# A two-layer diffusion step on one core: gate and up products of three feed-forward stages as seven block products in place of eight

## The chip, the cores and the metric

One Trainium2 chip, one of its cores. The metric is the device time of one launch in microseconds (us); the times shown are medians of runs, and lower is better. TensorE is called PE, VectorE DVE, ScalarE ACT, GpSimd POOL, and SyncE, which issues most transfers, SP. PEld stands for PE's loads of the stationary operand.

## What is computed

A backbone of two layers works on 640 tokens (128 context tokens, 512 latent ones) of 1024 features, all in float32. Each layer is a feed-forward stage, a mixer, and a second feed-forward stage:

```
x <- LN(alpha*x + 0.5*g1*SwiGLU_1(x*(1+s1)+b1))
x <- LN(alpha*x + g2*W_out[RG-LRU | GQA | MLA](x*(1+s2)+b2))
x <- LN(alpha*x + 0.5*g3*SwiGLU_2(x*(1+s3)+b3))

SwiGLU(u) = (silu(u @ w_gate) * (u @ w_up)) @ w_down      w_gate, w_up: 1024 x 2816, w_down: 2816 x 1024
mod = silu(cond) @ w_mod + b_mod                          nine sections of 1024 columns in each layer
```

The gates g, scales s and shifts b are sections of `mod`. There are four feed-forward stages, called f00, f01, f10 and f11 here (layer, then first or second), and two mixers, m0 and m1. The order of the program is f00, m0, f01, f10, m1, f11.

## The kernel before

**Products.** Every float32 operand of a large product is kept as two parts, hi (rounded to the PE's float32r format) and lo (the rest), and a product is three matmuls: hi by hi, hi by lo, lo by hi (`mm3`, lines 516 to 518). An **m-tile** is 128 of the 2816 hidden features, so a stage has 22. For one m-tile the gate product runs over 8 blocks of K and two halves of 320 tokens, three matmuls each, and so does the up product: 2 x 8 x 2 x 3 = 96 matmuls of 128x320. They accumulate in PSUM tiles of two banks (`p2`, three of them). The gate goes through silu on ACT (line 593), is multiplied by the up product on DVE (598) and is split into hi and lo (600, 601).

**Down products.** After every chunk of three or four m-tiles (`CHUNKS`) the function `down` runs ten groups (5 token tiles x 2 halves of the 1024 columns) of three matmuls of 128x512 for each m-tile (lines 809 to 811), in two one-bank PSUM tiles (`p1`). Each group is multiplied by the stage's gate on DVE (815) and added to the residual `x` on POOL (817), in the last chunk on DVE, with the statistics of the layer norm behind it (457).

**Weights.** A weight block of 512 KB is loaded by SP into a ring of `NR` = 4 raw tiles (`raw`), and split: a cast on ACT gives hi (175), a subtraction on DVE gives lo (180). The ring's slot is free after the split. Loads are taken in the order of the steps (`feed`).

**Modulation.** Sections of later stages are computed while a feed-forward stage runs: for each of 8 row blocks of w_mod, four DVE operations of 128x512 (lines 318 and 320). `PLAN` says which stage computes which sections: f00 five, f01 four, f10 four, f11 none; one section each falls into m0 and m1, on PE there.

**Order.** The program is a list of `Step`s. `run` emits the body of a step, and at each of its yields also one of the waiting splits of the next step that has some, so that weights are ready a little ahead; each engine then keeps an order that the framework's scheduler fixes when the kernel is built. At the start of a stage the residual is rescaled on DVE (lines 1916 and 1917), and stored to DRAM only ahead of a mixer (`spill`). At the program's start, 16 small transfers of per-layer vectors (`vrows`, lines 264 to 271) go out on POOL's own queue, while SP issues the loads of x, of the condition vectors (`crow`) and of the first weights.

## Time and profile before

| | |
|---|---|
| time of three runs | 2614.26, 2616.35, 2619.17 us (median 2616.35) |
| profiled execution | span 2615.8 us from first to last instruction; its own time is not listed apart, and its span lies 0.55 us below the median of the runs |
| busy: PE, DVE, ACT, POOL | 97%, 58%, 33%, 25% of the span |
| granted PE clock | full speed (tenths: 9 in each slice) |
| traffic | 272.80 MB, mean 104 GB/s |
| instructions | 39802, of them 16392 matmul records |

How to read it: a matmul's record is longer than the time after which the next one starts, because matmuls are pipelined, so what one costs is the distance between two starts. DVE's records overlap a little in the same way. The table of stretches gives the busy time of each engine by stage.

### The profile page before, as it was taken

The numbers are of one execution on the slowest core, as the hardware profiler recorded it, in microseconds if no ns is written. First come the engines' busy times: TensorE is split into PE (matmuls) and PEld (weight loads), VectorE is DVE, ScalarE is ACT, GpSimd is POOL, SyncE is SP. The second block draws the span as 40 slices with busy tenths as digits, with TensorE's granted clock in tenths as the row PEclk, the third lists the DMA queues.
The fourth block names the chain that finished last, engine by engine and source line by source line (L and its number), as shares of the span: only waits on it lengthen the run. The fifth ranks groups of instructions, "written<-read, shape, count | busy, mean of one in ns | idle before, by whom it ended". The sixth has DMA issues, their size and how long they took to land.

```text
span 2615.8 us, 39802 instructions
## 1 busy us (share of the span) xinstructions
PE 2532.2 (97%) x16392; PEld 2309.0 (88%) x16392; DVE 1519.1 (58%) x2332; ACT 860.3 (33%) x1315; POOL 643.7 (25%) x581
## 2 busy tenths in 40 slices
PE   8899999988999999999999999999999999999997
PEld 7799999888679889999988999998986899999996
DVE  5855765668656755545576636545786565323335
ACT  3312221356772322111242212214657542212211
POOL 4311022126433121121022211022363232210112
PEclk9999999999999999999999999999999999999999
DMA  7634543331221543333324424331330323223211
GB/s 273 187 96 141 160 130 106 92 98 54 88 77 59 173 121 105 100 111 113 114 64 154 126 77 145 114 113 46 99 106 26 114 87 97 73 65 97 73 57 41
DMA packets 266149, 272.80 MB, mean 104 GB/s; under 512 B 13236, under 2 KB 223728, under 8 KB 265968
## 3 DMA queue, kind: packets, MB, share of 16 engines
q1 hardware_dynamic: 265456, 270.18, 33.6%
q8 instruction: 129, 2.11, 0.3%
q14 instruction: 52, 0.43, 0.0%
q0 software_dynamic: 512, 0.08, 0.0%
HBM read 260.30 MB, written 8.34 MB: 103 GB/s over the span
## 4 chain that ended last, share of the span: by engine, by line
PE 57%; DVE 8%; issue 4%; ACT 2%; DMA 2%; POOL 1%; DVEq 0%; POOLq 0%; ACTq 0%; SPq 0%
PE p L516 12%; PE p L517 12%; PE p L518 12%; PE p L809 5%; PE p L810 5%; PE p L811 5%; PE p L1424 3%; PE p L1462 3%; PE p L1496 2%; DVE x L320 1%; DVE x L1916 1%; DVE x L1917 1%; DVE t L815 1%; DMA raw<-in_ffn_w_down 1%; DVE w L180 1%
## 5 line engine op out<-in xcount | busy, mean ns | idle before, releaser
L516 PE MATMUL p<-u,w 128*128 128x320 f32 (+2 forms) x2928 | 910.6, 311 | 2.7 <-ACT uf L502 1.5
L517 PE MATMUL p<-u,w 128*128 128x320 f32 (+2 forms) x2928 | 908.6, 310 | 3.0 <-POOL u L508 2.2
L518 PE MATMUL p<-u,w 128*128 128x320 f32 (+2 forms) x2928 | 907.3, 310 | 1.2 <-DVE w L180 1.2
L817 POOL TENSOR_TENSOR x<-x,t 128x512 f32<-128x512 f32 x200 | 273.7, 1371 | 1229.4 <-DVE t L815 1226.2
L516 PEld LDWEIGHTS p<-u,w 128*128 128x128 f32 x2928 | 552.1, 189 | 9.5 <-issue 2.9
L517 PEld LDWEIGHTS p<-u,w 128*128 128x128 f32 x2928 | 552.1, 189 | 6.4 <-POOL u L508 3.9
L518 PEld LDWEIGHTS p<-u,w 128*128 128x128 f32 x2928 | 552.0, 189 | 1.9 <-DVE w L180 1.8
L175 ACT CAST w<-raw 128x1024 fp32r<-128x1024 f32 x211 | 221.9, 1051 | 750.5 <-PE p L517 531.6
L180 DVE TENSOR_TENSOR w<-raw,w 128x1024 fp32r<-128x1024 f32 x211 | 263.0, 1248 | 222.1 <-ACT w L175 218.9
L809 PE MATMUL p<-dw,b 128*128 128x512 f32 x880 | 347.1, 394 | 14.8 <-DVE t L815 14.8
L810 PE MATMUL p<-dw,b 128*128 128x512 f32 x880 | 343.1, 390 | 0.0
L811 PE MATMUL p<-dw,b 128*128 128x512 f32 x880 | 342.7, 390 | 0.0
L320 DVE SCALAR_TENSOR_TENSOR x<-raw,cst,x 128x512 f32<-128x512 f32 x364 | 274.5, 805 | 48.4 <-DMA raw<-in_w_mod 48.0
L815 DVE TENSOR_TENSOR t<-p,g 128x512 f32<-128x512 f32 x240 | 164.6, 686 | 230.8 <-PE p L811 227.6
L175 ACT CAST dw<-raw 128x1024 fp32r<-128x1024 f32 x90 | 92.7, 1051 | 559.8 <-PE p L810 426.0
L809 PEld LDWEIGHTS p<-dw,b 128*128 128x128 f32 x880 | 165.2, 188 | 59.2 <-DVE t L815 24.7
L598 DVE TENSOR_TENSOR b<-b,p 128x640 f32<-128x640 f32 (+2 forms) x89 | 70.9, 796 | 222.4 <-PE p L518 222.2
L811 PEld LDWEIGHTS p<-dw,b 128*128 128x128 f32 x880 | 165.2, 188 | 35.2 <-DVE b L601 0.3
L810 PEld LDWEIGHTS p<-dw,b 128*128 128x128 f32 x880 | 165.3, 188 | 32.1
L180 DVE TENSOR_TENSOR dw<-raw,dw 128x1024 fp32r<-128x1024 f32 x90 | 118.6, 1328 | 112.7 <-ACT dw L175 112.7
L1487 POOL TENSOR_SCALAR b<-b,sm 128x640 f32<-128x640 f32 x96 | 78.3, 817 | 143.2 <-DVE sm L1477 60.6
L1476 DVE TENSOR_REDUCE sm<-p 128x1 f32<-128x640 f32 x96 | 78.9, 821 | 56.3 <-PE p L1462 52.9
(325 smaller groups left out, 3249.0 us busy)
## 6 DMA issues: line engine op xcount, KB each, us to landing
raw<-in_w_mod SPq DMA_DIRECT2D x132, 512.0 KB
raw<-in_ffn_w_gate SPq DMA_DIRECT2D x88, 512.0 KB
raw<-in_ffn_w_up SPq DMA_DIRECT2D x88, 512.0 KB
raw<-in_ffn_w_down SPq DMA_DIRECT2D x88, 512.0 KB
raw<-in_w_in SPq DMA_DIRECT2D x26, 512.0 KB
raw<-in_w_out SPq DMA_DIRECT2D x16, 512.0 KB
wm<-in_w_mod SPq DMA_DIRECT2D x12, 512.0 KB
xd<-x SPq DMA_DIRECT2D x10, 512.0 KB
```

The costliest lines, as they stand in the source:

```text
L175: nc.scalar.copy(h, hold["raw"])
L180: nc.vector.tensor_sub(l, hold["raw"], f(hold["hi"]))
L320: e.scalar_tensor_tensor(acc[:, cs], hold["raw"][:, cs], c, acc[:, cs], op0=ALU.mult, op1=ALU.add)
L516: nc.tensor.matmul(out, lhsT=wh, rhs=xh, start=start, stop=False)
L517: nc.tensor.matmul(out, lhsT=wh, rhs=xl, start=False, stop=False)
L518: nc.tensor.matmul(out, lhsT=wl, rhs=xh, start=False, stop=stop)
L809: nc.tensor.matmul(pt, lhsT=hh[:, ts], rhs=d["hi"][:, hsl], start=(i == 0), stop=False)
L810: nc.tensor.matmul(pt, lhsT=hh[:, ts], rhs=d["lo"][:, hsl], start=False, stop=False)
L811: nc.tensor.matmul(pt, lhsT=hl[:, ts], rhs=d["hi"][:, hsl], start=False, stop=(i == len(ms) - 1))
L815: nc.vector.tensor_mul(tt, pt, gt[h])
L817: e.tensor_add(x[:, hsl], x[:, hsl], tt)
L1476: nc.vector.tensor_reduce(st[:, 0:1], v, axis=AX.XY, op=ALU.max, negate=True)
```

## The change

Three stages (f01, f10, f11) are built by a new function `ffn_fast`; f00 keeps the old one. In `ffn_fast` the first two m-tiles (`CLASSIC` = 2) are computed as before. For the other 20, the 1024 inputs (K) are cut in two halves, the 640 tokens in two halves of 320, and the pair (gate, up) is the third cut, so that an m-tile is a 2 x 2 by 2 x 2 block product, done in **seven** block products of 4 blocks of K x 320 tokens (84 matmuls for 96). It needs sums of blocks of u once a stage (`sums`, `third`), four differences of weight halves for each m-tile, in place in the raw tiles on POOL (`prep`), splits of half the old width, and additions of results in PSUM (`keep_x`, `keep_q`, `fix`, `up1`). Weights are split up to three steps ahead (`LOOK`). Down products always follow three m-tiles (the last four) and are summed in SBUF tiles `acc`; the gate and the residual, which is now stored to DRAM in every stage, come in once, by `blend`, on POOL. Of the sections of modulation f00 now computes seven, f01 and f10 three each, f11 one and m1 none. The ring has five raw tiles, and the 16 transfers of `vrows` move from POOL's queue to ACT's.

```diff
-NR = 4
+NR = 5
 PLAN = {
-    "f00": [[], [], [(0, 3), (0, 4), (0, 5), (0, 6), (0, 7)]],
+    "f00": [[], [], [(0, 3), (0, 4), (0, 5), (0, 6), (0, 7), (1, 0), (1, 1)]],
-    "f01": [[], [], [(1, 0), (1, 1), (1, 2), (1, 3)]],
-    "f10": [[], [], [(1, 4), (1, 5), (1, 6), (1, 7)]],
-    "m1": [[], [(1, 8)]],
-    "f11": [[], [], []],
+    "f01": [[], [], [(1, 2), (1, 3), (1, 4)]],
+    "f10": [[], [], [(1, 5), (1, 6), (1, 7)]],
+    "m1": [[], []],
+    "f11": [[], [], [(1, 8)]],
+NX = 8
+LOOK = 3
+CLASSIC = 2
...
-            nxt = next((todo[k] for k in range(i + 1, len(steps)) if steps[k].splits), deque())
+            near = [todo[k] for k in range(i + 1, min(len(steps), i + 40)) if steps[k].splits][: s.look]
...
-            q = nc.gpsimd
+            q = nc.scalar
...
+    def ffn_fast(self, l, j, mods):
...
+                def whole(h, ts):
+                    t = B().rearrange("p (k n) -> p k n", k=2)
+                    nc.gpsimd.tensor_add(t, f(uh[h][:, ks, ts]), f(ul[h][:, ks, ts]))
+                    return t
...
+        def prep(m, key):
...
+            def op():
+                nc.gpsimd.tensor_sub(at(src), at(sub[0]), at(sub[1]))
+
+            def hi():
+                w = pairs[m, key] = self.W([P, 2, 4, P])
+                nc.scalar.copy(w[:, 0], at(src))
+
+            def lo():
+                w = pairs[m, key]
+                nc.vector.tensor_sub(w[:, 1], at(src), f(w[:, 0]))
+                if key in ("U2", "T4"):
+                    self.raw_out -= 1
...
+        def product(m, key, q, start, after=None, extra=()):
...
+                for k in range(4):
+                    xh, xl = a(k)
+                    out = bank(m, q)
+                    for i, (a1, b1) in enumerate(((w[:, 0, k], xh), (w[:, 0, k], xl), (w[:, 1, k], xh))):
+                        nc.tensor.matmul(
...
+            def keep_x():
+                tmp[m] = B()
+                nc.scalar.copy(tmp[m][:, H0], bank(m, X))
+
+            def keep_q():
+                nc.scalar.copy(tmp[m][:, H1], bank(m, Q))
+
+            def fix():
+                nc.vector.tensor_add(bank(m, Z), bank(m, Z), tmp[m][:, H0])
+                nc.scalar.copy(tmp[m][:, H0], bank(m, Z))
+                nc.vector.tensor_add(bank(m, Q), bank(m, Q), tmp[m][:, H0])
+
+            return [
+                product(m, "G1", X, True, keep_x, extra.get(0, ())),
+                product(m, "T1", Q, True, keep_q, extra.get(1, ())),
+                product(m, "T2", Z, True, fix, extra.get(2, ())),
+            ]
...
+            def up1():
+                nc.vector.tensor_add(tmp[m][:, H1], bank(m, Z), tmp[m][:, H1])
...
+            return [
+                product(m, "G2", X, False, gate0, extra.get(0, ())),
+                product(m, "T3", Z, False, up1, extra.get(1, ())),
+                product(m, "U2", Q, False, h0, extra.get(2, ())),
+                product(m, "T4", Z, False, h1, extra.get(3, ())),
+            ]
...
+        def blend():
...
+                    nc.sync.dma_start(out=xin, in_=env["x_d"][t][:, cs])
+                    yield
+                    nc.gpsimd.tensor_mul(acc[t][:, cs], acc[t][:, cs], g[:, cs])
+                    yield
+                    nc.gpsimd.tensor_add(acc[t][:, cs], acc[t][:, cs], xin)
...
+                        if begin:
+                            nc.scalar.copy(x[:, cs], pt)
+                        elif last:
+                            tt = T()
+                            nc.vector.tensor_mul(tt, pt, env["gate"][1 if t == 0 else 0][:, cs])
+                            nc.vector.tensor_add(x[:, cs], x[:, cs], tt)
+                            self.ln_part(t, h, 2)
+                        else:
+                            nc.vector.tensor_add(x[:, cs], x[:, cs], pt)
...
+        while n + 2 < NM:
+            a, b, c = n, n + 1, n + 2
...
+            S += part_a(a, {2: dw[0:1]} if n > CLASSIC else {})
+            S += part_a(b, {0: dw[1:2], 2: dw[2:3]} if n > CLASSIC else {2: dw})
+            S += mods.get(a, [])
+            S += part_b(a)
+            S += part_a(c)
+            S.append(down([a - 2, a - 1, a], begin=n == CLASSIC))
+            if n + 5 >= NM:
+                S.append(Step([], [], start_blend))
+            S += mods.get(b, [])
+            S += part_b(b) + mods.get(c, []) + part_b(c)
+            n += 3
```

Three places of the order show what moves. The number behind a name is its buffer; [waits ...] names what the instruction waits for, DMAHWn being the n-th of eight marks that transfers of SP and ACT take in turn.

First, SP's queue at the program's start. Before:

```order
L281 DMA x_78<-in_x_sample 128x512
L281 DMA x_79<-in_x_sample 128x512
L231 DMA crow<-in_c 8x128
L232 DMA crow<-in_c_ctx 8x128
L233 DMA crow<-in_b_mod 16x128
L170 DMA raw_150<-in_ffn_w_gate 128x8x128 [waits DMAHW0_49]
L1963 DMA wm_130<-in_w_mod 128x2x512 [waits DMAHW1_49]
L1963 DMA wm_131<-in_w_mod 128x2x512 [waits DMAHW2_49]
L1963 DMA wm_132<-in_w_mod 128x2x512 [waits DMAHW3_49]
L1963 DMA wm_133<-in_w_mod 128x2x512 [waits DMAHW4_49]
```

and now:

```order
L285 DMA x_77<-in_x_sample 128x512
L285 DMA x_78<-in_x_sample 128x512 [waits DMAHW0_49]
L285 DMA x_79<-in_x_sample 128x512 [waits DMAHW3_49]
L235 DMA crow<-in_c 8x128 [waits DMAHW5_49]
L236 DMA crow<-in_c_ctx 8x128 [waits DMAHW7_49]
L237 DMA crow<-in_b_mod 16x128 [waits DMAHW1_49]
L173 DMA raw_150<-in_ffn_w_gate 128x8x128 [waits DMAHW3_49]
L2344 DMA wm_130<-in_w_mod 128x2x512 [waits DMAHW0_49]
L2344 DMA wm_131<-in_w_mod 128x2x512 [waits DMAHW2_49]
L2344 DMA wm_132<-in_w_mod 128x2x512 [waits DMAHW3_49]
```

Before, nine transfers go out with no wait, and the first weight load is the first that waits. Now ACT's 16 transfers take marks from the same eight, and SP waits from its fourth transfer on, `crow` and the weights behind it.

Second, DVE between two down chunks. Before, in f01 (180 lo of a weight block, 598 and 601 the hidden features, 374 the end of a modulation section):

```order
L598 TENSOR_TENSOR b_8848<-b_8848,p_1274_9046 128x640
L180 TENSOR_TENSOR w_9204<-raw_9148,w_9188 128x1024
L601 TENSOR_TENSOR b_9109<-b_8848,b_9108 128x640
L180 TENSOR_TENSOR w_9293<-raw_9206,w_9279 128x1024
L180 TENSOR_TENSOR dw_9622<-raw_9357,dw_9604 128x1024
L598 TENSOR_TENSOR b_9119<-b_9119,p_1289_9175 128x640
L374 TENSOR_TENSOR modsb_9260<-p_1299_9251,bm_97 128x256
```

and now, in f11 (1048 lo of a half block, 1101 and 1103 `fix`, 1117 `up1`, 1120 and 1125 the hidden features, 324 modulation):

```order
L1048 TENSOR_TENSOR w_22191<-raw_21943,w_22191 128x512
L1101 TENSOR_TENSOR p_2926_21036<-p_2926_21036,b_22117 128x320
L1048 TENSOR_TENSOR w_22204<-raw_21943,w_22204 128x512
L1103 TENSOR_TENSOR p_2925_21035<-p_2925_21035,b_22117 128x320
L324 SCALAR_TENSOR_TENSOR x_21164<-raw_22168,cst,x_21164 128x512 x2
L324 SCALAR_TENSOR_TENSOR x_21165<-raw_22168,cst,x_21165 128x512 x2
L1048 TENSOR_TENSOR w_22234<-raw_21818,w_22234 128x512
L1101 TENSOR_TENSOR p_2926_21036<-p_2926_21036,b_22182 128x320
L1048 TENSOR_TENSOR w_22250<-raw_22210,w_22250 128x512
L1103 TENSOR_TENSOR p_2925_21035<-p_2925_21035,b_22182 128x320
L1117 TENSOR_TENSOR b_22117<-p_2926_21036,b_22117 128x320
L1048 TENSOR_TENSOR w_22270<-raw_22210,w_22270 128x512
```

The half blocks' splits now stand between the additions in PSUM, and PE's T4 waits for 1117, PE's next products for 1101 and 1103.

Third, POOL ahead of the last down chunk of f01. Before it only added the chunk to x:

```order
L817 TENSOR_TENSOR x_7626<-x_7626,t_9030 128x512
L817 TENSOR_TENSOR x_7626<-x_7626,t_9043 128x512
L817 TENSOR_TENSOR x_7618<-x_7618,t_9469 128x512
L817 TENSOR_TENSOR x_7618<-x_7618,t_9482 128x512
L817 TENSOR_TENSOR x_7620<-x_7620,t_9495 128x512
```

and now (1040 differences of weight halves, 1145 the gate's factor 0.5, 1155 and 1157 `blend`):

```order
L1040 TENSOR_TENSOR raw_11754<-raw_11781,raw_11754 128x512
L1145 TENSOR_SCALAR x_12029<-x_12029 128x1024
L1040 TENSOR_TENSOR raw_11754<-raw_11754 128x512
L1155 TENSOR_TENSOR x_9150<-x_9150,x_12029 128x512
L1157 TENSOR_TENSOR x_9150<-x_9150,t_12036 128x512
L1155 TENSOR_TENSOR x_9150<-x_9150,x_12029 128x512
...
L1155 TENSOR_TENSOR x_9154<-x_9154,x_12026 128x512
L1157 TENSOR_TENSOR x_9154<-x_9154,t_12199 128x512
L1040 TENSOR_TENSOR raw_11796<-raw_11905,raw_11796 128x512
L1040 TENSOR_TENSOR raw_11905<-raw_11905 128x512
```

The twenty operations of `blend` stand as one block, with the differences of m-tile 20 (the last two rows) behind them.

## Rows read from the trace of the kernel before

**Rows 1.** The page's busy line: engine, busy us, share, instructions.
```profile
PE 2532.2 (97%) x16392; PEld 2309.0 (88%) x16392; DVE 1519.1 (58%) x2332; ACT 860.3 (33%) x1315; POOL 643.7 (25%) x581
```
**Rows 2.** Stretches f00, f01, f10, f11: length; busy PE, PEld, DVE, ACT, POOL; PEclk, DMA.
```profile
0.00:530.00 530.00, 507.46 (x3351) 462.90 (x3351) 339.01 (x518) 139.46 (x189) 118.83 (x114) 1.00 0.47 146
...
855.00:1340.00 485.00, 475.79 (x2886) 442.03 (x2885) 281.27 (x384) 121.62 (x159) 88.94 (x71) 0.99 0.37 113
1340.00:1821.00 481.00, 474.21 (x2885) 441.27 (x2884) 277.19 (x381) 117.92 (x156) 88.10 (x72) 1.00 0.37 110
...
2142.00:2602.00 460.00, 458.85 (x2753) 430.82 (x2751) 183.07 (x222) 101.27 (x118) 81.79 (x66) 1.00 0.24 74
```
**Rows 3.** Timeline of PE, gate products in f00: start, length, instruction.
```profile
299.74 0.31 PE L516 MATMUL p<-u,w 128*128 128x320 f32 x1
...
305.90 0.31 PE L516 MATMUL p<-u,w 128*128 128x320 f32 x1
```
**Rows 4.** Timeline of PE, down products in f01.
```profile
980.28 0.39 PE L809 MATMUL p<-dw,b 128*128 128x512 f32 x1
...
984.36 0.39 PE L809 MATMUL p<-dw,b 128*128 128x512 f32 x1
```
**Rows 5.** Groups of DVE: operation, shapes, count | busy us, mean ns | idle before.
```profile
L180 DVE TENSOR_TENSOR w<-raw,w 128x1024 fp32r<-128x1024 f32 x211 | 263.0, 1248 | 222.1 <-ACT w L175 218.9
L815 DVE TENSOR_TENSOR t<-p,g 128x512 f32<-128x512 f32 x240 | 164.6, 686 | 230.8 <-PE p L811 227.6 <-POOL x L817 3.1
...
L601 DVE TENSOR_TENSOR b<-b,b 128x640 fp32r<-128x640 f32 x86 | 70.8, 824 | 1.6 <-ACT b L600 1.6
...
L1849 DVE TENSOR_TENSOR b<-p,b 128x256 f32<-128x256 f32 x40 | 16.8, 419 | 13.2 <-PE p L518 9.8 <-issue 3.1
```
**Rows 6.** Groups of ACT.
```profile
L506 ACT CAST u<-uf 128x512 fp32r<-128x512 f32 x50 | 30.9, 618 | 1.3
...
L1525 ACT CAST b<-p 128x256 fp32r<-128x256 f32 x24 | 9.1, 378 | 5.1 <-PE p L1424 5.1
```
**Rows 7.** Groups of POOL.
```profile
L817 POOL TENSOR_TENSOR x<-x,t 128x512 f32<-128x512 f32 x200 | 273.7, 1371 | 1229.4 <-DVE t L815 1226.2 <-DVE spt L1056 1.9 <-DVE spt L1053 1.2
...
L2016 POOL TENSOR_TENSOR u<-b,u 128x640 fp32r<-128x640 f32 x8 | 13.8, 1745 | 23.2 <-ACT u L2014 23.2
```
**Rows 8.** Timeline of DVE in f01 with POOL idle.
```profile
957.77 3.40 DVE L320 SCALAR_TENSOR_TENSOR x<-raw,cst,x 128x512 f32<-128x512 f32 x5
```
**Rows 9.** Timeline of DVE and POOL in f00's first down chunk.
```profile
108.51 0.68 DVE L815 TENSOR_TENSOR t<-p,g 128x512 f32<-128x512 f32 x1
...
109.11 2.44 DVE L320 SCALAR_TENSOR_TENSOR x<-raw,cst,x 128x512 f32<-128x512 f32 x2
...
109.27 1.74 POOL L817 TENSOR_TENSOR x<-x,t 128x512 f32<-128x512 f32 x1 [1.76 <-DVE t L815]
...
111.48 0.68 DVE L815 TENSOR_TENSOR t<-p,g 128x512 f32<-128x512 f32 x1
```
**Rows 10.** Who waited for whom on PE, first 75 us of f01.
```profile
PE p L809 <- DVE t L815: 2.4, 4, 0.7
```
**Rows 11.** The same, first 75 us of f10.
```profile
PE p L809 <- DVE t L815: 3.2, 4, 1.4
```
**Rows 12.** Timeline of SP and PE at the program's start.
```profile
3.81 0.32 SPq L233 DMA_DIRECT2D crow<-in_b_mod  x1
4.17 0.42 SPq L170 DMA_DIRECT2D raw<-in_ffn_w_gate  x1
...
7.94 0.28 PE L249 MATMUL p<-ident,crow 32*128 32x32 f32 x1 [7.94 <-DMA crow<-in_b_mod]
```
**Rows 13.** DMA issues: operation, count, KB each, us to landing.
```profile
vrows<-in_ln_g POOLq DMA_DIRECT2D x2, 12.0 KB, 4.7
```
**Rows 14.** Chain of waits in f01: start, us, what.
```profile
902.33 4.67 DMA raw<-in_ffn_w_gate
```

More of the change, by code (lines that the diff above doesn't have):

```diff
@@ L100, with __init__ @@
 class Step:
-    def __init__(self, loads=(), splits=(), body=lambda: iter(()), cap=99):
-        self.loads, self.splits, self.body, self.cap = list(loads), list(splits), body, cap
+    def __init__(self, loads=(), splits=(), body=lambda: iter(()), cap=99, look=1):
+        self.loads, self.splits, self.body, self.cap, self.look = list(loads), list(splits), body, cap, look
 class Kern:
@@ L142, in X @@
     def X(self, shape, dt=F32):
-        return self.pp.tile(shape, dt, tag="X", bufs=7, name=self.nm("x"))
+        return self.pp.tile(shape, dt, tag="X", bufs=NX, name=self.nm("x"))
     def U(self, shape, dt=F32R):
@@ L211, in run @@
                 cap += more or 0
+                nxt = next((q for q in near if q), None)
                 if nxt and cap and self.ahead and nxt[0].ready():
@@ L659, in biased @@
                             )
-                r = self.tiny([4, 2, P], "brow")
+                r = B()[0:4, 0 : 2 * P].rearrange("p (i n) -> p i n", i=2)
                 nc.vector.tensor_copy(r, pb[0:4, 0 : 2 * P].rearrange("p (i n) -> p i n", i=2))
@@ L872, in H, with tiny @@
             return env["pool"].tile([P, 2304], F32, tag="H", bufs=2, name=self.nm("h"))
-        def tiny(shape, tag):
-            return self.tiny(shape, tag, 2)
+        def tiny(shape, tag, bufs=1):
+            return env["pool"].tile(shape, F32, tag=tag, bufs=bufs, name=self.nm(tag))
         def open_pool():
@@ L886, in consts @@
             for n, w in (("gqa_q_norm", 64), ("gqa_k_norm", 64), ("mla_q_norm", 192), ("mla_kv_norm", 128)):
-                t = self.tiny([P, w], n, 1)
+                t = tiny([P, w], n)
                 nc.sync.dma_start(out=t, in_=I[n][l : l + 1, :].to_broadcast([P, w]))
@@ L1095, in qk_post @@
             nc.scalar.activation(sq, xn, AF.Square)
-            ss = tiny([P, 2, 10], "ssq")
+            ss = tiny([P, 2, 10], "ssq", 2)
             nc.vector.tensor_reduce(
@@ L1472, in softmax @@
                 fa = factor(h0 + r, 1 + 2 * qq + q)
-                st = self.tiny([P, 4], "sm", 6)
+                st = tiny([P, 4], "sm", 6)
                 v = ps_.pop(u)[:, :, 0:HALF]
@@ L1561, in att_prompt @@
             v = ps.rearrange("p (h w) -> p h w", h=nh)
-            st = tiny([P, 3, 4], "smp")
+            st = tiny([P, 3, 4], "smp", 2)
             nc.vector.tensor_reduce(st[:, 0, 0:nh], v, axis=AX.X, op=ALU.max)
@@ L1875, in end_tile @@
             self.sb = self.scale_shift(*self.next_mod)
-            self.spill = self.next_mod[1] == 1
+            self.spill = True
             self.new_u = self.u_alloc()
-        g = LN_LAG[self.spill]
+        g = LN_LAG[0]
         if t >= g:
@@ L1989, in mod_half @@
                     self.raw_out -= 1
-            sb = self.tiny([P, P], "mhsb")
+            sb = self.tiny([P, P], "modsb")
             nc.vector.tensor_copy(sb, ps[:, 0:P])
@@ L2056, in begin, with spread @@
             yield
-        def spread(plan, m_from=0):
+        def spread(plan, m_from=0, m_to=NM):
             r = {}
-            for secs, m0, m1 in zip(plan, (0, 1, m_from), (1, 3, NM)):
+            for secs, m0, m1 in zip(plan, (0, 1, m_from), (1, 3, m_to)):
                 q = [st for ls in secs for st in self.mod_steps(*ls, late="v")]
@@ L2084, in go @@
             steps.append(setnext((l, 2) if self.skip_mixer else (l, 1)))
-            plan = spread(PLAN[f"f{l}0"], 3 if l == 0 else 0)
-            new = self.ffn_steps(l, 0, plan)
+            plan = spread(PLAN[f"f{l}0"], *((3,) if l == 0 else (2, 18)))
+            new = self.ffn_steps(l, 0, plan) if l == 0 else self.ffn_fast(l, 0, plan)
             if l == 0:
@@ L2096, in go @@
                 steps.append(Step([], [], states))
-            steps += self.ffn_steps(l, 1, spread(PLAN[f"f{l}1"]))
+            steps += self.ffn_fast(l, 1, spread(PLAN[f"f{l}1"], 2, 18))
         self.run(steps)
```

239 lines of the change are left out of this document (238 added, 1 removed).

## The prediction

> **What bounds the kernel now.** I read the busy line first [rows 1]: PE is busy for 97% of the span, DVE for 58%, ACT and POOL for a third or less. A busy PE says little by itself, since matmul records overlap, so next came what a matmul really takes, the distance between two starts. Among the gate products it is (305.90 - 299.74) us over 42 starts = 0.1467 us [rows 3], among the down products (984.36 - 980.28) / 18 = 0.2267 us [rows 4], at a granted clock of 1.00 [rows 2], the upper of its two levels, 2.4 GHz. Then the stretches by stage [rows 2]. A feed-forward stage has 22 x 96 = 2112 matmuls of 128x320 and 660 of 128x512: 309.8 + 149.6 = 459.4 us by these distances. The stretch of f11 is 460 us long. So there PE never waits, and f01 and f10 (485 and 481 us) hold some 20 us more, most of it at the turn of a stage. In the long middle of a stage PE alone sets the time; that is where the change takes work away, and the whole question is what the other engines do when PE asks for its weights and banks sooner.
>
> **What is removed.** 20 m-tiles of three stages have 84 matmuls in place of 96: 720 fewer, x 0.1467 = **105.6 us** less [rows 3]. The down products keep their number. The 32 small matmuls of the section that leaves m1 run beside the attention there and I cost them at nothing.
>
> **What is added, by period.** In the new stages three m-tiles and one down chunk repeat. On PE a period is 252 x 0.1467 + 90 x 0.2267 = 37.0 + 20.4 = 57.4 us. On DVE it holds:
> - 21 splits of half blocks. Five 128x512 operations in a row took 3.40 us, 0.68 each [rows 8]: 14.3 us.
> - 3 splits of down weights at 1.25 (L180) [rows 5]: 3.7 us.
> - 15 operations of 128x320 on PSUM. No row has this width; 128x256 took 419 ns and 128x512 686 ns (L1849 and L815) [rows 5], and by their line I take 0.49: 7.4 us. That `fix` also writes PSUM no row shows; the same two rows bound it, 0.42 to 0.69.
> - 3 lo parts of the hidden features at 0.82 (L601) [rows 5]: 2.5 us, and 10 down sums at 0.69 (L815) [rows 5]: 6.9 us.
>
> That is 34.8 us. Modulation comes on top: three sections in f01 and f10 are 24 blocks over 16 m-tiles, 4.5 blocks of four operations in a period, 12.2 us; one section in f11, 4.1 us. So DVE needs 47 of 57.4 us in f01 and f10 and 39 in f11. POOL has 12 differences at 1.37 [rows 7], 16.4 us, in place of 10 additions. ACT has 21 casts at 0.62 (L506) [rows 6], 15 reads of 128x320 between 0.38 and 0.62, by the line of the two rows 0.44 (L1525 and L506) [rows 6] and a few casts more, some 25 us. No engine passes PE over a period.
>
> But the work is not spread over the period. Splits run three products ahead at most, so in the down chunk (20.4 us) DVE has its 6.9 us of sums and some modulation, and the rest must fit into the 37.0 us of products: 40 us in f01 and f10, 32 in f11, with a lag of three products, 3 x 12 x 0.1467 = 5.3 us, that the next down chunk makes good. Taken alone DVE would just do it.
>
> **DVE and POOL in turn.** In f00's first down chunk two 128x512 operations of DVE with both operands in SBUF meet an addition of POOL [rows 9]: DVE's pair, 1.36 us by rows 8, held it from 109.11 to 111.48, 1.0 us longer, and POOL's addition took 1.74 against a mean of 1.37 [rows 7]. The operation that reads PSUM took its usual 0.68 at 111.48. So the two engines take turns on such work, and each meeting costs DVE up to 1.0 us. Before, a chunk's ten additions met DVE in its idle time; now 12 differences in each period stand in the 37 us in which DVE is full. Bounds: no meeting, 0; all of them, 12 us a period. I take one in three, 4 us, because the differences wait for DVE's own previous split and can run while DVE does its 15 operations on PSUM, and because the mean of 1.37 shows that most additions so far met nothing. Then f01 and f10 have 44 us for 42.3 us: 1.7 us lost in each of five periods, **17 us** for both stages (bounds 0 and 100), and f11 loses nothing.
>
> **The start of a stage.** From the first product to the second down chunk PE has 28.2 (two old m-tiles) + 22.9 + 20.4 + 37.0 = 108.5 us. DVE has the residual (20 x 0.69 [rows 5]), the sums (16 x 0.82), 39 half splits, 24 operations on PSUM, some 11 splits and products of the old kind and 30 of modulation: 98 us, beginning some 10 us behind PE; POOL adds 8 sums at 1.75 (L2016) [rows 7] and 22 differences, of whose 30 meetings a third costs 10 us. 98 + 10 + 10 - 108.5 - 5.3 = 4, say **6 us** for f01 and f10 together (bounds 0 and 50). What goes is the wait of the first down chunk for DVE, which was 2.4 us in f01 [rows 10] and 3.2 in f10 [rows 11]: **-5.6 us**; ACT now reads that chunk.
>
> **The wait that is new.** T4 writes the bank that `up1` reads, and only U2, 12 x 0.1467 = 1.76 us, lies between T3 and T4. Behind it in PE's order stand T4, then all the next m-tile; ahead of `up1` on DVE may stand a split in hand of 0.68 or 1.25 us, with a meeting 1.0 more, and `up1` takes 0.49. So T4 is late by 0 to 1.25 + 1.0 + 0.49 - 1.76 = 1.0 us. I take 0.3 for each of 60 m-tiles, near the lower end since a plain 0.68 leaves room: **18 us** (0 to 60).
>
> **Edits at the edges.** At the start SP issued `crow` and the first weights by 4.6 us without a wait, and PE began at 7.94 us when `crow` landed [rows 12]. Now SP waits from its fourth transfer on for marks which ACT's 16 small transfers also hold; such a transfer took 4.7 us to land [rows 13], so I take **+4 us** (0 to 10). f00 has 16 more blocks of modulation, so more meetings like rows 9 at its down chunks: **+2 us** (0 to 7). The block of 20 operations of `blend` (27 us of POOL) stands ahead of m-tile 20's differences, but 20.4 us of down chunk and 14.1 us of products lie between: hidden; without them it would cost up to 27 us a stage. The 15 MB of stores and loads of the residual are hidden by transfers that are busy 24 to 37% in these stages [rows 2].
>
> **The sum**, against the profiled span of 2615.8 us: -105.6 + 17 + 6 - 5.6 + 18 + 4 + 2 = -64.2, so 2551.6; the median of the runs stands 0.55 us above the span. **I forecast 2552 us.** The five losses are 47 together; with all of them at half or at one and a half times, its own range is 2528 to 2576.
>
> **Rivals.**
> - *Nothing is lost.* Splits stay three products ahead and the meetings fall into gaps: 2615.8 - 105.6 + 4 - 5.6 + 0.55 = **2509 us** (to 2525 with a few waits). For it: f11 before is packed without a gap [rows 2]. Against it: DVE goes from about half to over 80% of f01 and f10.
> - *The ring of five raw tiles.* Gate and up blocks are now held until T4. With the order A(a) A(b) B(a) A(c), down, B(b) B(c) (A three products, 5.3 us; B four, 7.0), a load of 4.7 us [rows 14] and the splits, m-tile a holds its two tiles some 22 us, b 50, c 45: 2 x 117 = 234. Down weights take 3 x 7 = 21 and modulation 4.5 x 8 = 36 more in f01 and f10: 291 of 5 x 57.4 = 287 tile-us. The ring is booked out there (f11: 267), so a load goes out only when a tile falls free and PE waits part of 4.7 + 0.62 + 0.68 = 6.0 us for it: 3.5 us in some 11 periods, 38 us on the forecast, **2590 us**.
> - *Slower: DVE and POOL meet always.* Each POOL operation that reads SBUF holds up DVE by the full 1.0 us of rows 9: 52 us for 42.3 in f01 and f10, 9.7 us in each of ten periods, 98 + 10 + 30 - 113.8 = 24 at each of their starts, and some 16 in f11: 161 us where I took 23. 2552 + 138 = **2690 us**. It decides the sign from about two meetings in three on: from a third on each further tenth of the meetings costs about 21 us, so the 64 us of the forecast are gone near 0.64. The Trainium skill's page "SBUF — State Buffer", section "Who interferes with whom", says that a VectorE instruction with two SBUF inputs contends with a GpSimd instruction that reads SBUF, and that the second one to issue fully blocks. By that rule, the trace agrees: 1.0 us in rows 9, and none for the operation on PSUM; what it leaves open is how often the two meet.
>
> **Chances.** The forecast 0.52, nothing lost 0.14, the ring 0.20, always meeting 0.11 and 0.03 for something else. Some 0.2% (5.2 us) is what a measurement of this kernel can tell from no change. Faster by more: all of the first two and most of the ring's share, 0.82; within it: 0.05, from the ring's upper end and a share of meetings near two in three; slower: 0.13. The range leaves out the lowest end of the first rival and the last one: **2514 to 2620 us**.
>
> **What would show it.** The matmul count falls by about 744 and the distance stays 0.1467; f11 is shortest, some 35 us under 460. In f01 and f10 DVE is over 80% busy between down chunks. Waits of PE on DVE lines 1117 and 1048 carry most of what is lost; if they stand on the loads of gate and up instead, it is the ring; if half splits take 1.7 us in the mean, it is the meetings. A PE clock under full speed in these stages, or a wait for the blend, would be outside of all this and make the forecast wrong.

## The result, and the profile after

The changed kernel takes **2785.55 us** in the median (2783.67 to 2790.0), the kernel before 2615.51 us beside it: a ratio of 1.0648, with an interval of 1.0632 to 1.0663. Faster by 64 us was forecast; it is slower by 170 us and lies outside the range. The matmuls went as they were to, the rest did not. Of the page of the changed kernel, the busy line, which answers to [rows 1]:

```profile
PE 2501.8 (90%) x15624; PEld 2238.0 (80%) x15624; DVE 1936.6 (70%) x2952; ACT 1077.6 (39%) x1909; POOL 935.4 (34%) x733
```

There are 768 matmul records fewer, yet PE went from 97% to 90%. The stretches f00, f01, f10 and f11 (columns as in [rows 2]):

```profile
0.00:551.00 551.00, 516.09 (x3387) 466.33 (x3387) 382.01 (x533) 135.53 (x182) 114.29 (x97) 0.99 0.50 157
...
876.00:1405.00 529.00, 462.69 (x2621) 417.48 (x2619) 384.37 (x543) 190.87 (x351) 186.57 (x125) 0.95 0.34 104
1405.00:1932.00 527.00, 464.00 (x2624) 418.88 (x2624) 381.22 (x544) 189.35 (x352) 185.99 (x130) 0.95 0.34 104
...
2258.00:2767.00 509.00, 445.29 (x2530) 405.15 (x2531) 341.03 (x452) 175.29 (x318) 181.98 (x122) 0.96 0.28 86
```

Against [rows 2], f01 is longer by 44 us, f10 by 46, f11 by 49, f00 by 21; the two mixers and the end together by 6. Two things here decide how to read on. The old stage f00 lost time as well. And f11, with one modulation section and DVE busy for 67%, lost as much as f01 and f10, with three sections and 73%: so it is not the amount of work on DVE alone. (Each of the three had 35.2 us of matmuls taken away, so the loss against them is that much more.) A period of three m-tiles, counted from the first product behind a down chunk, takes (2621.8 - 2425.9) / 3 = 65.3 us in f11, where its matmuls need 57.4. Who waited for whom on PE in f11 (us in total, times, longest):

```profile
PE p L1072 <- ACT b L1102: 17.5, 8, 4.5
PE p L1072 <- DVE b L1117: 14.7, 9, 5.3
PE p L1180 <- ACT b L906: 11.4, 1, 11.4
PE p L1072 <- ACT b L1095: 7.1, 5, 1.9
PE p L1072 <- DVE w L1048: 4.7, 3, 3.8
```

and over the whole span:

```profile
PE p L1072 <- ACT b L1102: 54.2, 22, 4.5
PE p L1072 <- DVE b L1117: 35.3, 20, 5.4
PE p L1180 <- ACT b L906: 34.0, 3, 11.4
PE p L1072 <- ACT b L1095: 18.6, 14, 1.9
```

L1117 is the wait that was foreseen; L1102 (the copy in the middle of `fix`) and L1095 (`keep_x`) were not. L906 belongs to the start of a stage. No load is among the waits in f11. Why do these short operations come late? The costliest groups over the whole span, a row each of DVE, ACT and POOL (what ended the idle time before them stands last):

```profile
L1048 DVE TENSOR_TENSOR w<-raw,w 128x512 fp32r<-128x512 f32 x420 | 348.2, 846 | 161.8 <-ACT w L1044 160.7
...
L1044 ACT CAST w<-raw 128x512 fp32r<-128x512 f32 x420 | 249.1, 620 | 292.6 <-POOL raw L1040 241.1 <-PE p L1072 42.0 <-DMA raw<-in_ffn_w_gate 4.8
...
L1040 POOL TENSOR_TENSOR raw<-raw,raw 128x512 f32<-128x512 f32 x120 | 180.3, 1502 | 626.7 <-DVE w L1048 480.1 <-DMA raw<-in_ffn_w_up 89.0 <-DVE p L1103 32.4
```

Read upwards, it is a chain: POOL's difference (1.5 us) waits for DVE's split, because the block is differenced in place; ACT's cast waits for the difference, 241 us in all; DVE's next split waits for the cast, 161 us in all. And each of these engines takes its work in order: while DVE stands at a split, what is behind it stands too. One turn from m-tile 8 to m-tile 9, timeline of f11:

```profile
2436.96 2.22 DVE L183 TENSOR_TENSOR dw<-raw,dw 128x1024 fp32r<-128x1024 f32 x1
...
2439.10 0.48 DVE L1117 TENSOR_TENSOR b<-p,b 128x320 f32<-128x320 f32 x1
...
2439.63 3.78 PE L1072 MATMUL p<-u,w 128*128 128x320 f32 x24 [1.21 <-DVE b L1117]
...
2441.90 1.29 POOL L1040 TENSOR_TENSOR raw<-raw,raw 128x512 f32<-128x512 f32 x1
2443.22 0.62 ACT L1044 CAST w<-raw 128x512 fp32r<-128x512 f32 x1 [3.95 <-POOL raw L1040]
...
2443.88 1.25 DVE L1048 TENSOR_TENSOR w<-raw,w 128x512 fp32r<-128x512 f32 x1 [2.70 <-ACT w L1044]
...
2445.45 2.32 DVE L183 TENSOR_TENSOR dw<-raw,dw 128x1024 fp32r<-128x1024 f32 x1
...
2447.76 0.42 ACT L1095 COPY b<-p 128x320 f32<-128x320 f32 x1
...
2448.23 2.03 PE L1072 MATMUL p<-u,w 128*128 128x320 f32 x12 [1.30 <-ACT b L1095]
...
2448.43 2.97 DVE L1048 TENSOR_TENSOR w<-raw,w 128x512 fp32r<-128x512 f32 x3
2449.19 1.66 POOL L1040 TENSOR_TENSOR raw<-raw 128x512 f32<-128x512 f32 x1 [2.50 <-DVE w L1048]
2451.32 0.48 DVE L1101 TENSOR_TENSOR p<-p,b 128x320 f32<-128x320 f32 x1
...
2451.89 0.43 ACT L1102 COPY b<-p 128x320 f32<-128x320 f32 x1 [2.35 <-DVE p L1101]
...
2452.37 4.83 PE L1072 MATMUL p<-s,w 128*128 128x320 f32 x19 [2.11 <-ACT b L1102]
```

`up1` (L1117) stands behind a down-weight split that met POOL (2.22 us in place of 1.25). ACT stands 3.95 us at a cast, DVE 2.70 us behind it. The first half of `fix` (L1101) is due at some 2446.8, where T2 ends; it comes at 2451.32, behind another down-weight split that met POOL (2.32 us) and three half splits of which one did (2.97 us for 3 x 0.68). And PE waits for `fix` and `keep_x` of m-tile 8 although its next products write the *other* bank: the waits that the built program holds go by whole tiles, and a tile of X, Q or Z has the banks of two m-tiles (experiment 1 bears this out).

The clock is the last loss. The stretch before that last wait ended, the one after it, and one a little later:

```profile
2448.20:2452.30 4.10, 2.03 (x12) 1.77 (x12) 4.10 (x6) 1.75 (x5) 1.66 (x1) 1.00 0.43 128
2452.30:2456.00 3.70, 3.56 (x12) 3.29 (x13) 3.70 (x7) 0.86 (x3) 0.00 (x0) 0.54 0.49 142
2457.80:2464.00 6.20, 6.20 (x44) 6.20 (x44) 4.06 (x7) 1.49 (x3) 3.59 (x3) 1.00 0.39 134
```

After PE had stood still for half of 4.1 us its granted clock was 0.54, near the lower level of 1.2 GHz, for the next 3.7 us (12 matmuls in the time of 25). Over the stages that is a mean of 0.95 to 0.96 in place of 0.99 to 1.00.

At the start of a stage the same three engines meet in another way. DVE, ACT and POOL in f01:

```profile
884.52 11.57 POOL L973 TENSOR_TENSOR b<-u,u 128x640 f32<-128x640 f32 x6
...
888.61 4.05 DVE L2297 SCALAR_TENSOR_TENSOR x<-x,gamma 128x512 f32<-128x512 f32 x2
...
905.38 0.68 DVE L2297 SCALAR_TENSOR_TENSOR x<-x,gamma 128x512 f32<-128x512 f32 x1
...
914.61 0.81 DVE L922 TENSOR_TENSOR b<-b,p 128x640 f32<-128x640 f32 x1
...
915.51 0.72 ACT L906 CAST b<-b 128x640 fp32r<-128x640 f32 x1 [2.60 <-DVE b L922]
...
923.04 0.68 DVE L1048 TENSOR_TENSOR w<-raw,w 128x512 fp32r<-128x512 f32 x1
```

PE reaches the first new product at 903.0 us. DVE still has the residual and the sums of hidden halves ahead, its first two rescalings at 2.0 us each beside POOL's sums, where one alone takes 0.68; the hidden features of m-tile 1 come at 915.5 and the lo part of the first new weights at 923. PE stands for most of these 20 us.

### The profile page after: what moved, and what is told of

The parts are those of the page before. It is cut to its first block, busy times and chain, and to the rows that moved or that the text cites. A ratio compares the mean times of both kernels' runs of the same rounds, so it can differ in the third digit from the quotient of the medians.

```text
span 2781.9 us, 40019 instructions
## 1 busy us (share of the span) xinstructions
PE 2501.8 (90%) x15624; PEld 2238.0 (80%) x15624; DVE 1936.6 (70%) x2952; ACT 1077.6 (39%) x1909; POOL 935.4 (34%) x733
## 5 line engine op out<-in xcount | busy, mean ns | idle before, releaser
L1072 PE MATMUL p<-u,w 128*128 128x320 f32 x2880 | 460.8, 316 | 66.5 <-DVE b L1117 35.3
L1072 PEld LDWEIGHTS p<-u,w 128*128 128x128 f32 x2880 | 436.3, 192 | 84.0 <-DVE b L1117 41.2
L1048 DVE TENSOR_TENSOR w<-raw,w 128x512 fp32r<-128x512 f32 x420 | 348.2, 846 | 161.8 <-ACT w L1044 160.7
L1072 PE MATMUL p<-s,w 128*128 128x320 f32 x2160 | 375.8, 328 | 63.9 <-ACT b L1102 53.7
L1072 PEld LDWEIGHTS p<-s,w 128*128 128x128 f32 x2160 | 347.1, 202 | 81.2 <-ACT b L1102 59.4
L1040 POOL TENSOR_TENSOR raw<-raw,raw 128x512 f32<-128x512 f32 x120 | 180.3, 1502 | 626.7 <-DVE w L1048 480.1
L1044 ACT CAST w<-raw 128x512 fp32r<-128x512 f32 x420 | 249.1, 620 | 292.6 <-POOL raw L1040 241.1
L520 PE MATMUL p<-u,w 128*128 128x320 f32 (+2 forms) x1008 | 317.8, 315 | 3.2 <-ACT uf L506 2.0
L521 PE MATMUL p<-u,w 128*128 128x320 f32 (+2 forms) x1008 | 315.8, 313 | 3.9 <-POOL u L512 3.8
L522 PE MATMUL p<-u,w 128*128 128x320 f32 (+2 forms) x1008 | 314.1, 312 | 0.0
L1180 PE MATMUL p<-dw,b 128*128 128x512 f32 x630 | 250.1, 397 | 49.5 <-ACT b L906 34.0
L1182 PE MATMUL p<-dw,b 128*128 128x512 f32 x630 | 248.2, 394 | 4.4 <-DVE b L907 4.2
L1181 PE MATMUL p<-dw,b 128*128 128x512 f32 x630 | 247.1, 392 | 0.0
L178 ACT CAST dw<-raw 128x1024 fp32r<-128x1024 f32 x87 | 90.5, 1048 | 354.6 <-PE p L1181 187.6
L1040 POOL TENSOR_TENSOR raw<-raw 128x512 f32<-128x512 f32 x120 | 177.7, 1481 | 117.7 <-DVE w L1048 113.0
L520 PEld LDWEIGHTS p<-u,w 128*128 128x128 f32 x1008 | 192.3, 191 | 8.0 <-ACT uf L506 2.6
L521 PEld LDWEIGHTS p<-u,w 128*128 128x128 f32 x1008 | 192.3, 191 | 6.4 <-POOL u L512 5.6
L522 PEld LDWEIGHTS p<-u,w 128*128 128x128 f32 x1008 | 192.1, 191 | 0.1
```

Of the source, the lines that this page charges most:

```text
L178: nc.scalar.copy(h, hold["raw"])
L520: nc.tensor.matmul(out, lhsT=wh, rhs=xh, start=start, stop=False)
L521: nc.tensor.matmul(out, lhsT=wh, rhs=xl, start=False, stop=False)
L522: nc.tensor.matmul(out, lhsT=wl, rhs=xh, start=False, stop=stop)
L1040: nc.gpsimd.tensor_sub(at(src), at(sub[0]), at(sub[1]))
L1044: nc.scalar.copy(w[:, 0], at(src))
```

## Experiments

Three theories were set against each other. **A:** the shared tiles make products wait for the other m-tile's readers. **B:** splits that wait in order for POOL's differences hold up the corrections. **C:** POOL's differences hold up DVE on SBUF. Beside them **S:** the start of a stage is a loss of its own.

**1. Six tiles of one bank (A).**
```diff
...
-            env["bank"] = [self.p2() for _ in range(3)]
+            env["bank"] = self.swap2(True)
...
-            return env["bank"][q][:, tiles[m], 0:HALF]
+            return env["bank"][q][tiles[m]][:, 0:HALF]
...
```

`p2` gives tiles of [P, 2, 512]; `swap2(True)` gives 3 x 2 tiles of [P, 512].

> Edit: the three PSUM tiles of two banks, which m-tiles share by halves, become six tiles of one bank, so that a product waits only for readers of its own bank; nothing is left out. Theory A (shared tiles): in the profile after the change G1 of an m-tile waits for the copy L1095 of the m-tile before it and T1 or T2 for its L1102 and L1103, which read the other bank of the same tile; 18.6 + 54.2 us of TensorE's waits stand on L1095 and L1102. They go, and some 20 us of lower clock after them: about 2690 us, 2670 to 2720. Theory B (order of the queues): the correction only stands late because VectorE and ScalarE wait in order for GpSimd's differences, so the wait moves on to T3, U2 and T4: 2750 to 2785 us.

2765.0 us, 20.5 us faster: A holds a small part. The waits on L1095 and L1102 (now L1106 and L1113) are gone from f11, and the time is now waited for at `up1` (now L1128):

```profile
PE pb L1083 <- DVE b L1128: 36.0, 12, 6.2
PE p L1192 <- ACT b L917: 11.4, 1, 11.4
PE pb L1083 <- DVE b L1131: 6.1, 2, 3.4
```

As B had said, the wait moves on (L1131 is `h0`).

**2. No differences, and differences on DVE (B and C against A).**
The first kernel leaves the differences out: T1 to T4 are formed from one block as it was loaded.
```diff
-            fns = [op, hi, lo] if sub else [hi, lo]
+            fns = [hi, lo]
```
The second has them on DVE:
```diff
-                nc.gpsimd.tensor_sub(at(src), at(sub[0]), at(sub[1]))
+                nc.vector.tensor_sub(at(src), at(sub[0]), at(sub[1]))
```


> Edit: the differences of weight blocks are left out (T1, T2, T3 and T4 are formed from one block as it was loaded); all casts, splits and products stay. Theory B (the chain difference on GpSimd, cast on ScalarE, rest on VectorE holds up what is queued behind it) and theory C (GpSimd's differences hold up VectorE on SBUF) both lose their cause: 2660 us or less in B, with half splits near 0.68 us in place of 0.846; in C the same fall only as far as VectorE was full, most in f01 and f10. Theory A (shared tiles): the correction chain VectorE, ScalarE, VectorE after T2 still ends later than G1 of the next m-tile, so most of the waits on L1102 stay: 2740 to 2780 us.

> Edit: the differences of weight blocks run on VectorE in place of GpSimd; nothing is left out. Theory C (meetings): no difference meets VectorE any more, half splits fall to 0.68 us, and VectorE takes 240 differences of 0.68 us = 163 us in exchange for some 70 us of slower splits: about 2750 to 2790 us, f11 gains, f01 and f10 not. Theory B (in-order queues wait for GpSimd): a difference is done 0.7 us sooner and without a hop, so what stands behind it on VectorE starts sooner: 2700 to 2750 us. Theory A: the waits for the other m-tile's bank stay: 2770 to 2800 us.

Without differences 2603.0 us; with all of them on DVE 2626.6 us, a gain of **159 us** from one word, more than any theory had put there, with the tiles shared as before. So A is not the main cause. The groups of DVE with the differences on DVE:

```profile
L1048 DVE TENSOR_TENSOR w<-raw,w 128x512 fp32r<-128x512 f32 x420 | 284.5, 699 | 43.6 <-ACT w L1044 43.0
...
L1040 DVE TENSOR_TENSOR raw<-raw 128x512 f32<-128x512 f32 x120 | 85.7, 716 | 1.0
L1040 DVE TENSOR_TENSOR raw<-raw,raw 128x512 f32<-128x512 f32 x120 | 85.3, 711 | 6.8 <-DMA raw<-in_ffn_w_up 4.9
```

DVE took 171 us more of work; its splits fell from 846 to 699 ns, its idle time in front of them from 161.8 to 43.6 us. A period of f11 takes (2477.0 - 2300.2) / 3 = 58.9 us. Both the meetings (C) and the waiting (B) had gone with that word, so the next runs took them apart.

**3. Meetings alone, and waiting alone.** The same number of POOL operations, behind the splits, into a tile that nobody reads:
```diff
                 nc.vector.tensor_sub(w[:, 1], at(src), f(w[:, 0]))
+                if sub:
+                    nc.gpsimd.tensor_sub(self.scr.rearrange("p (a b) -> p a b", a=4), f(w[:, 0]), f(w[:, 1]))
```


> Edit to the kernel with the differences on VectorE (2626.6 us, 159 us faster than the change): GpSimd gets as many operations of 128x512 on SBUF as it had differences, each behind the split of its product and into a tile that nobody reads; nothing is left out. Theory C (meetings): GpSimd's reading of SBUF is what cost the time; about a third of VectorE's splits take 1.16 us again and most of the 159 us comes back: 2720 us or more. Theory B (order): the time went because splits in VectorE's and ScalarE's order waited for GpSimd's result, and here nothing waits for it: 2626 to 2665 us, with the splits as slow as in the change.

> Edit to the kernel without differences (2603.0 us): GpSimd gets as many operations of 128x512 on SBUF as the change has differences, behind the splits and into a tile that nobody reads. As there, the differences themselves are left out. No engine waits for GpSimd, and VectorE has the same work as in the change, so this holds the meetings of the change alone, and what then lacks to 2785.6 us is the waiting for GpSimd's results in order. Theory C (meetings): 2720 us or more. Theory B (order): 2605 to 2650 us. After the run with idle operations on GpSimd beside differences on VectorE (2778.8 us, where VectorE also had the differences) I expect both to hold a part, 2660 to 2700 us.

And a later cast with nothing on POOL:
```diff
                 nc.vector.tensor_sub(at(src), at(sub[0]), at(sub[1]))
+                nc.scalar.copy(at(src), at(src))
+                nc.scalar.copy(at(src), at(src))
```


> Edit to the kernel with the differences on VectorE (2626.6 us): ScalarE copies each differenced block onto itself twice before the cast, 2 x 0.62 us, so that a difference reaches its cast 1.2 us later, as with GpSimd (1.49 us for 0.71 us, and a hop between engines), with no operation on GpSimd; nothing is left out. Theory B (order): what stands behind the splits on VectorE waits again, 2680 us or more. Theory C: no meeting comes with it, 2626 to 2650 us; ScalarE has 15 us more in a period of 57 us, of which it used about half.

The idle operations beside differences on DVE brought 2778.8 us: nearly all of the 159 us came back, which I had expected of C only. Without differences they cost 2710.3 - 2603.0 = **107 us**, and the change lies **75 us** above that. The delay alone took 2682.5 us, 56 us more. So both mechanisms are shown, each nearly without the other. Meetings cost some 107 us (an upper end, since the idle operations met more splits, see below); ACT and DVE stood only 4.9 us in all for an idle operation. Waiting in order cost 56 us where a delay alone made it, and some 75 us as what the change has beyond the meetings. The 56 us are less clean: the two copies also gave ACT 257 us more work in these stages, in the same queue as the copies of `fix`. The split of the kernel without differences, of that with the idle operations and no differences, then of the delayed one:

```profile
L1048 DVE TENSOR_TENSOR w<-raw,w 128x512 fp32r<-128x512 f32 x420 | 293.1, 710 | 73.1 <-ACT w L1044 71.7
```

```profile
L1049 DVE TENSOR_TENSOR w<-raw,w 128x512 fp32r<-128x512 f32 x420 | 394.7, 953 | 60.9 <-ACT w L1045 59.6
```
```profile
L1050 DVE TENSOR_TENSOR w<-raw,w 128x512 fp32r<-128x512 f32 x420 | 290.1, 721 | 102.9 <-ACT w L1046 102.6
```

With the idle operations the splits are slow, and the idle time in front of them is no longer than without; with the delay they are quick, and it is more than double that of dve_diff (43.6). Counted one by one in the trace, 145 of the change's 420 splits overlap a POOL operation and take 1155 ns in the mean, the other 275 take 683; with the idle operations 197 do.

The stretch f11 (columns as in [rows 2]) without differences, with them on DVE, with the idle operations alone, and in the change:

```profile
2138.20:2588.00 449.80, 431.41 (x2526) 398.29 (x2525) 297.31 (x449) 175.07 (x314) 63.16 (x41) 0.97 0.31 97
...
2151.70:2612.00 460.30, 433.40 (x2526) 399.53 (x2524) 341.27 (x531) 172.70 (x314) 63.57 (x42) 0.97 0.30 95
...
2208.70:2688.00 479.30, 440.33 (x2527) 403.63 (x2525) 340.64 (x450) 174.23 (x314) 186.89 (x121) 0.97 0.29 91
...
2260.30:2768.00 507.70, 444.94 (x2527) 404.57 (x2524) 339.73 (x451) 173.38 (x314) 181.13 (x122) 0.96 0.27 86
```

**4. More lead.** `LOOK = 3` became 5.

> Edit to the change: LOOK = 5 in place of 3, so that the differences, casts and splits of a product are issued up to five products ahead; the differences stay on GpSimd and nothing is left out. Theory B: a difference, its cast and split take 3 us one behind the other and three products are 5.3 us; two products more of lead take most of the wait out of the queues: 2700 us or less. Theory C: the same operations meet as often as before: 2770 to 2790 us. Rival within B: the longer lead puts still more splits ahead of L1101 and L1117 in VectorE's order, and the time rises.

2798.4 us, 13 us slower, as the rival within B had it: lead does not help where the chain is in the order itself, and it lets more splits stand ahead of `fix` and `up1`. That it is this and not the meetings is not shown: the splits also grew to 885 ns.

**5. The start (S).** `CLASSIC = 5`: five plain m-tiles, a down chunk after the third.
```diff
-CLASSIC = 2
+CLASSIC = 5
...
+            if m == 2:
+                dl, dsp = down_w(2)
+                S[-1].loads.append(dl)
+                S += [Step([], dsp), down([0, 1, 2], begin=True)]
...
```


> Edit: five m-tiles instead of two are done the old way at the start of each of the three stages, with a down chunk after the third; the 36 matmuls a stage that the new way saves there come back, 3 x 36 x 0.1467 = 15.8 us. Theory S (start): the 25 us of waits in the first 66 us of each stage come from VectorE, which has the residual and the sums of hidden halves ahead of the first new products; with 42 us more of plain products ahead they go: 2785 + 16 - 3 x (15 to 22) = 2735 to 2755 us. Rival: the same waits come whenever the new products begin, because the differences start only then: 2785 to 2805 us.

> Edit to the kernel with the differences on VectorE (2626.6 us): five plain m-tiles at the start of each of the three stages, 15.8 us more of matmuls; nothing is left out. If the start is a loss apart from the differences (34 us of waits for the hidden features of m-tile 1 stand there, with 4.2 us a stage more behind it), 46 us go and 16 come back: 2590 to 2605 us. If the start's loss only moves, 2625 to 2645 us.

On the change 2730.5 us, 55 us faster in spite of 15.8 us more of matmuls; but there it also takes nine m-tiles out of the slow periods. With the differences on DVE it is the cleaner reading: 2611.4 us, 15 us faster, so 31 us went with the start. Some 5 of them are the three periods that it saves there too, each of 58.9 us for 57.4; the rest was a loss of the start's own.

**6. The sections in f00.** In the kernel with the differences on DVE, (1, 0) and (1, 1) moved back to f01: four sections each in f01 and f10.

> Edit to the kernel with the differences on VectorE: the modulation sections (1, 0) and (1, 1) go back from f00 to f01 (f00 five sections, f01 and f10 four each, f11 one); nothing is left out. The first stage is 21 us longer than before, of which 5.4 us stand at its first product. If the two sections there are the rest, f00 falls by 10 to 16 us from 551; f01 and f10 then carry 16 operations more of 32 each and grow by what VectorE lacks there, 5 to 25 us together. If f00 stays at 545 us or more, the rest is in the start and what it shifts.

2623.2 us (2618.0 to 2627.4), 3 us less, about its spread; but the stage answers. The last transpose behind f00 starts at 552.6 us in the kernel with the differences on DVE and at 538.3 here: the two sections cost **14 us** there. Half of this went again in the later stages: f01, f10 and f11 took 480, 474 and 463 us in place of 477, 473 and 460, though f11's work had not changed.

**7. Together.** Edits 1, 2 (on DVE) and 5; with 6; with the sums of hidden halves on DVE too; and the tiles alone.

> Three edits to the change together: differences on VectorE, six PSUM tiles of one bank, five plain m-tiles at the start of a stage; nothing is left out. Alone they gave -159, -20 and -55 us. If the start's wait is apart from the steady part, the first and third add up, and of the second something is left: 2555 to 2575 us, which would be faster than the kernel before. If the differences on VectorE already took the start's wait, or VectorE is now full, 2600 to 2630 us.

> The three edits that gave 2607.5 us (differences on VectorE, six PSUM tiles of one bank, five plain m-tiles) with the modulation sections of f00 and f01 back: f00 falls by 14 us as in the run before, f01 and f10 give 4 to 10 us back: 2597 to 2604 us; over 2607 us if VectorE is full in f01 and f10 with four sections.

> As the kernel beside it, and the eight sums of hidden halves at the start of each stage run on VectorE in place of GpSimd (24 x 2.4 us there, 24 x 0.81 us on VectorE): theory C says that the residual next to them gets 1 us an operation shorter for some eight operations, so the start of a stage gains 1 to 5 us: 2585 to 2600 us. If VectorE's own load counts there, no gain or up to 6 us a stage lost.

> Edit to the kernel with the differences on VectorE (2626.6 us): six PSUM tiles of one bank in place of three of two; nothing is left out. If the shared tiles cost only while the corrections come late, as the profile with the differences on VectorE says (L1102 there holds 8.0 us of waits in place of 54.2, L1095 none): 2615 to 2630 us. If they cost 20 us by themselves, as in the change: 2600 to 2610 us.

They took 2607.5, 2609.5, 2607.6 and, the tiles alone on dve_diff, 2635.0 us. So the shared tiles cost 20 us while the corrections came late and nothing once they came in time (the own tiles were 8 us slower there, which no run explains). The gains did not add up: of 20 and 55 us about 19 were left. Then the lead again, in the kernel of all edits:

> The kernel with five edits (2607.6 us) and LOOK = 4. With the differences on VectorE a split's lead could be worth something at the turns of the down chunk; but each product of lead puts more splits ahead of the corrections on VectorE, and in the change LOOK = 5 cost 13 us. I expect 2605 to 2620 us.

> The same kernel with LOOK = 2: fewer splits stand ahead of the corrections on VectorE. If the queue in front of the corrections is what is left, 2590 to 2604 us; if the lead is short, the products wait for their splits, 2615 us or more.

2605.9 us with `LOOK` = 4 (0.9962 of the kernel before, 0.995 to 0.9974) and 2610.1 with 2: no difference beyond their spread. The stretches f00, f01, f10 and f11 with 4:

```profile
0.00:539.00 539.00, 512.00 (x3351) 468.04 (x3351) 332.40 (x461) 135.55 (x182) 109.44 (x97) 0.98 0.47 145
...
863.00:1338.00 475.00, 453.93 (x2684) 415.35 (x2685) 399.19 (x631) 183.76 (x331) 51.31 (x38) 0.98 0.42 126
1338.00:1809.00 471.00, 453.23 (x2674) 415.80 (x2672) 393.67 (x635) 179.83 (x323) 48.86 (x41) 0.98 0.41 125
...
2135.00:2590.00 455.00, 436.30 (x2558) 404.28 (x2557) 322.91 (x497) 164.59 (x289) 45.65 (x32) 0.98 0.31 96
```

This beats both kernels, the one before by 0.4%, where its matmuls alone (612 fewer, 90 us) would give over 3%: DVE is now busy for 84% of f01 and f10, and in all these stretches the clock is at 0.98.

## Why the prediction was wrong, step by step

- **What bounds the kernel, and what is removed: right.** In the timeline of the changed kernel 24 matmuls of 128x320 still start within 3.5 us (2425.95 to 2429.46), and the 720 matmuls went. Without differences, and so nearly without waits, a period of f11 takes (2458.0 - 2284.5) / 3 = 57.8 us, where 57.4 was worked out. The count fell by 768 and not by 744: the section that left m1 had 64 small matmuls and not 32, and f11 has 16 for it.
- **The failed step is "DVE and POOL in turn", +17 us.** It was too small, and it became time in another way. Its share was one in three of the 12 differences in a period, at 1.0 us each: 4 us. (145 of 420 is a share of the splits, and not this one.) In the trace 185 of the 240 differences overlap a DVE operation with both operands in SBUF, and DVE's busy time in f11 is 339.7 us against 297.3 without differences: 42 us, or 6.4 in each of 6.7 periods; in f01 and f10 it is 5.6 and 5.9. By the prediction's own sum this would have cost f01 and f10 some 35 us in place of 17, and f11 still nothing. But f11, forecast at some 425 us, took 509, and the idle operations alone cost it 29.5 us (449.8 to 479.3). The meetings were charged to DVE's sum over a period, only where that sum ran over. DVE is not a sum but an order, and PE waits for single short operations in it.
- **Inside that step stood the sentence that hid the rest:** the differences "can run while DVE does its 15 operations on PSUM". They seldom do: 53 of 240 overlap one, for 22 us of POOL's 358. Those operations often stand *behind* the split that waits for the difference. The Trainium skill's page "PSUM — Partial Sum Buffer", section "Engine vs sequencer instructions", says that the queues of ScalarE and VectorE are strictly first in, first out; the trace agrees, with 2.70 us of DVE and 3.95 us of ACT at one cast. Nothing was put in the sum for this waiting in order; it took some 75 us. And three of the 15, the products of L1125, have both operands in SBUF: 46 of all 60 met POOL, at 0.82 us in the mean against 0.48.
- **Rows 9 do not show what is read in them of PSUM.** The addition there had ended at 111.01 us when the operation on PSUM began at 111.48. The changed kernel shows it: `up1` takes 0.48 us in the 17 cases with POOL beside it and 0.48 in the 43 without.
- **"The wait that is new", +18 us:** the mechanism was right and the size was not. L1117 holds 35.3 us in all. The bound of 1.0 us a time allowed one split ahead of `up1`; the longest wait was 5.4 us.
- **Not in the sum: `fix` of one m-tile ahead of products of the next.** The waits on L1102 and L1095 are 54.2 + 18.6 us in all; they are the same lateness, seen through shared tiles, and giving them tiles of their own took 20 us off the time.
- **"The start of a stage", +6 and -5.6 us:** measured at 31 us, of which some 5 are not the start's own. The sum of DVE's work up to the second down chunk was about right (in f01 DVE is busy for 110.7 us from 877 to 1024 us, where 98 and 10 for meetings had been put); what decided was that the residual and the sums stand ahead of the *first* new split. The first down chunk's wait did not go: it is 11.4 us in each stage, for ACT's L906 behind DVE's L922.
- **"Edits at the edges":** +4 us was about right (the first gate product starts at 22.46 us in place of 17.08, 5.4 later). The two sections in f00, +2 us with a bound of 7, took 14.
- **The blend, put at nothing:** near it PE waits 5.3 to 5.4 us for `up1` of m-tile 19 in each stage. In f11 POOL's last sum ends at 2701.05 and the difference behind it at 2702.30; the split of that block and a down-weight split that met POOL stand ahead of `up1`. With the differences on DVE it still waits 3.4 us; there the sums draw DVE's differences out to 1.67 us.
- **The clock** was named as outside of all this, and it was: 0.95 to 0.96 in the three stages.
- **The rivals.** *DVE and POOL meet always* had the right sign and the right pair of engines, but not the mechanism. By its scale, on which all meetings are 12 us in a period, the measured 5.6 to 6.4 us are about a half, under the 0.64 from which its sum gives a slower kernel; the waiting in order, which it does not have, came on top. *The ring of five raw tiles* did not happen: no wait of PE on a load is in these stages. POOL stood 89.0 us until a load of up weights landed, but PE's waits soon behind these are 1.3 us at most, and with the differences on DVE 4.9 us of DVE's idle time in front of them ends with a load.

Together: the differences on POOL 159 us (35 had been put down for them and for `up1`), the start 31, f00's sections 14. The kernel without any differences lies 92 us over the kernel before less 105.6; beside the start, the sections and the first product some 40 of these are left that no run here accounts for; part of it is the clock (0.97 to 0.98 in its stages) and 5 us stand in the mixer m1.

## What to carry to other kernels

Where an engine has slack over a period, look at what stands *in front of* the short operations that the bounding engine waits for: a queue in order turns the latency of another engine's result into a wait for everything behind it. An operation given to an idle engine is not free if its result returns into such a queue or if both engines contend for SBUF: here the idle engine's 1.49 us against 0.71 us on the busy one made 159 us. And the waits of the built program show whether two halves of a buffer are really apart.

## What the runs showed of the hardware that was not expected

- A DVE operation on SBUF that met a POOL operation took 1155 ns in the mean against 683 alone, and 2.0 us where POOL ran one operation after another (L2297 at 888.61). The Trainium skill's page "SBUF — State Buffer", section "Who interferes with whom", has the second to issue fully blocked; the trace agrees for the two in a row, 2.0 us is about what one of POOL's six took there (11.57 / 6 = 1.9).
- The same added busy time on DVE cost very different times: in f11 44 us of differences on DVE took 10.5 us (449.8 to 460.3), 43 us of longer operations from meetings took 29.5. Why a lengthened operation costs three times as much as an added one was not settled.
- PE's granted clock fell to 0.54 after two waits of 1.30 and 2.11 us, with 2.03 us of work between them, and a stage with many of them kept 0.95 in the mean.
